# Double blocks of seven products in the first feed-forward, on rows scaled in place

## The chip, the core and the metric

The kernel runs on one core of a Trainium2 chip. Five engines work side by side, each through its own instructions in order: TensorE (PE, matmuls), VectorE (DVE), ScalarE (ACT), GpSimd (POOL) and SyncE (SP), which issues the DMA transfers. They wait for each other by semaphores. The metric is the device time of one execution in microseconds; before the change it is 1522.33 us, the median of 3 runs (1522.22 to 1524.28).

## What is computed

A decoder trunk of two layers on 256 rows of 1024 numbers, all in float32:

```
for i in range(2):
    x = x + 0.5 * swiglu(rmsnorm(x, norm_ffn1[i]), w_ffn1_up[i], w_ffn1_down[i])
    h = rmsnorm(x, norm_mix[i])
    x = x + token_mixers(h, ...)                      # three branches, gates, w_out
    x = x + 0.5 * swiglu(rmsnorm(x, norm_ffn2[i]), w_ffn2_up[i], w_ffn2_down[i])
    gate = sigmoid(rmsnorm(x, norm_ple[i]) @ w_ple_gate[i])
    x = x + gate * (p[i] @ w_ple_proj[i])
return rmsnorm(x, norm_final)

def rmsnorm(x, g): return x * rsqrt(mean(x * x) + 1e-6) * g
def swiglu(x, w_up, w_down):                          # w_up 1024 x 5632, w_down 2816 x 1024
    g, u = split(x @ w_up, 2)
    return (silu(g) * u) @ w_down
```

The change concerns the first line of layer 0.

## The kernel before

Every product is made of three matmuls of a faster type (L227 to L229): each operand is split into a part h, rounded to that type, and the rest l, and h·h, l·h and h·l are added in PSUM. A weight unit is 128 x 1024 numbers (512 KB): SyncE loads it into one of four buffers raw, ScalarE casts it to h (L221), VectorE subtracts (L222, l = raw - h). The h and l tiles come from pools of five, and of two more (ph, pl) while the wide pools are open. The rows of the input, transposed, are kept as xth and xtl, one pair for each half t of 128 rows.

A feed-forward runs over 11 blocks of 256 hidden numbers. A narrow block has 48 up matmuls (four units, two halves of rows), silu and product (hid: sg on ScalarE, hd on VectorE), the 24 down matmuls of the block before, and four transposes of hd (L468) whose result is split again (fh, fl). The last block transposes in two steps (L542). A wide, or double, block does two neighbouring blocks at once: a 2 x 2 product of matrices with seven products instead of eight, 84 up matmuls instead of 96. For this VectorE sums quarters of the weights (L385), ScalarE and VectorE split each sum (L377, L378), and four sums of the rows (sums_x) are split once in each feed-forward.

Three of the four feed-forwards have wide blocks at 2, 5 and 8. Their rows are normalised before they are split: xs is x times rstd (L300 on ScalarE, L301 on VectorE), eight transposes (L311) bring it into PSUM, VectorE multiplies by the gains into xr (L314), and ScalarE and VectorE split xr into xth and xtl. The first feed-forward of layer 0 gets x transposed from memory, multiplies by the gains alone, starts its matmuls before the rows' norm is known, and multiplies by rstd behind the product, in hid (L462, L463). Its eleven blocks are all narrow, and its wide pools are not open.

rstd comes from jk (L426: the squares' sum, ScalarE), ms (L431, VectorE) and a power on POOL (L432).

Between layer 0 and layer 1 stands the gate of the layer's embedding (ple): four products sq of 24 matmuls, one for each half of columns and rows; for each a sigmoid g on ScalarE (L596), a product with pp (L597) and the sum into x on VectorE (L598), and jk. Behind the third the first half of the rows is complete, and ms, rstd, xs and its transposes follow for the next feed-forward, whose first units are cast in the same stretch. In layer 1 the gate is the last step but the final norm.

The order on each engine is not written out by hand. A scheduler sets it from the order in which the program asks for work, from priorities and from the buffers that are free; the pools' rotation runs through the whole program.

Of the kernel before, what the change touches and what calls it, by code (L numbers as in the profile page):

```python
# [10 lines left out]
F32 = mybir.dt.float32  # L11
# [4 lines left out]
OP = mybir.AluOpType  # L16
# [6 lines left out]
FB = DFF // 256  # L23
# [41 lines left out]
SPLIT_AHEAD = 0  # L65
WIDE = (2, 5, 8)
LANES = {'a': 1, 'b': 1, 'c': 2}
# [16 lines left out]
def plan(name, i):  # L84
    if (name, i) == ("w_ffn1", 0):
        return [(False, b) for b in range(FB)]
    return [(b in WIDE, b) for b in range(FB) if b - 1 not in WIDE]

# [56 lines left out]
class Build:  # L145
# [183 lines left out]
    def mixer_open(self):  # L329
        self.scope = ExitStack()  # L330
        for n, bufs in (("ar1", 1), ("ar2", 1), ("pp_", 3), ("gt", 6)):
            setattr(self, n, self.scope.enter_context(self.tc.tile_pool(name=n, bufs=bufs, reuse_waits="tile")))

    def sums_x(self):
        nc = self.nc
# [101 lines left out]
    def ffn(self, name, gcol_next, mid=None, hook=None):  # L437
        nc = self.nc
        rstd = self.rstd
        scaled = (name, self.layer) != ("w_ffn1", 0)  # L440
        acc = {}
# [42 lines left out]

        for wide, b in plan(name, self.layer):
            if wide:
                hds = self.wide_up(name, b)
                downs()
                prev = []
                for j in range(2):  # L490
                    hh = self.fh.tile([128, 2, 256], F32R, name="fh")
                    ll = self.fl.tile([128, 2, 256], F32R, name="fl")
                    pt = self.pt.tile([128, 2, 256], F32, name="pt")
# [21 lines left out]
            for q, t in order:  # L515
# [4 lines left out]
                up(q, t)  # L520
            hds = [hid(pu, t) for t in range(2)]
            if b < FB - 1:
                if prev is not None:
# [4 lines left out]
                self.hl(hh, ll, pt)  # L528
                if scaled and b == 0:
                    self.sums_x()  # L530
            else:
# [614 lines left out]
    def constants(self):  # L1146
        nc, a = self.nc, self.a
# [21 lines left out]
        self.cols = cols = dict(zip(GAINS, (0, 16, 32, 48, 64, 80, 86)))  # L1169
        self.g_cq, self.g_ckv = cols["c_q_norm"], cols["c_kv_norm"]  # L1170
        self.mhalf = self.const.tile([128, 4], F32, name="mhalf")
        nc.vector.memset(self.mhalf, -0.5)
# [36 lines left out]
    def program(self, out):  # L1209
# [5 lines left out]
        cols = self.cols  # L1215
        self.norm_begin(cols["norm_ffn1"])

        def load_xt(t):
# [8 lines left out]
        def late(b):  # L1227
            if b == 2:
                self.load_consts()
                nc.gpsimd.dma_start(self.mask_b, a["const_i"])  # L1230
                self.load_gnorm()
                self.bounds()
# [14 lines left out]
        for i in range(DEPTH):  # L1247
            self.layer = i
            self.ffn("w_ffn1", cols["norm_mix"] + 8 * i, hook=self.late_loads if i == 0 else None)
            if i:  # L1250
                self.wide_close()
            self.mixer_open()
# [67 lines left out]
```

## Time and profile before

| | us |
|---|---|
| median of 3 runs | 1522.33 |
| profiled execution | 1522.07 |
| its span | 1519.8 |
| PE busy | 1490.3 (98%) |
| DVE busy | 1106.9 (73%) |
| ACT busy | 935.1 (62%) |
| POOL busy | 39.0 (3%) |
| DMA queue of SyncE | 263.00 MB, 51.5% of 16 engines' span |

A row of the timeline shows the start in us from the span's begin, the duration, engine, line, operation, output and inputs, shape, and how many such instructions follow each other; in brackets the idle time of the engine before it and what ended it. Matmuls overlap: a matmul of 128 x 512 shows a duration of 0.39 us, and the next one starts 0.23 us later. One row of a matmul in plain float32 stands for two records ("x2").

### The profile page before, as it was taken

To read this page: it belongs to the slowest core of one execution; us is meant where nothing else is said; L and a number is where in the kernel's file an instruction comes from. 1 tells how busy PE (TensorE), PEld (TensorE's weight loads), DVE (VectorE), ACT (ScalarE), POOL (GpSimd) and SP (SyncE) were. 2 spreads that over 40 slices of the span, in tenths; PEclk is the share of its full clock that TensorE was granted. 3 is DMA by queue.
4 is the path that set the end of the run, shared out by engine and by line. 5 is a ranking of instruction groups with operands and counts; after the bars stand their busy time and mean duration, and the time that the engine had idled before them with its cause. 6 is when DMAs were issued, how large, how long until landed. Compare 5 with 4: busy or idle time off the path is not lost.

```text
span 1519.8 us, 21607 instructions
## 1 busy us (share of the span) xinstructions
PE 1490.3 (98%) x8176; PEld 1242.5 (82%) x8176; DVE 1106.9 (73%) x1657; ACT 935.1 (62%) x1373; POOL 39.0 (3%) x48
## 2 busy tenths in 40 slices
PE   8999999999999999999989999999999999999997
PEld 6888888888888878888868888888888888788886
DVE  6555577677866679997679996776777666899965
ACT  6444486578655466756756665865885644666655
POOL 0000010000000000000000000100000000000000
PEclk9999999999999999999989999999999999999999
DMA  8665545454537652458534435553445285544462
GB/s 292 194 195 190 179 142 189 121 170 121 177 113 259 211 189 104 184 216 286 166 110 172 181 146 187 160 182 117 150 149 166 97 301 178 172 162 183 166 216 70
DMA packets 76472, 264.53 MB, mean 174 GB/s; under 512 B 8608, under 2 KB 9536, under 8 KB 76368
## 3 DMA queue, kind: packets, MB, share of 16 engines
q1 hardware_dynamic: 76144, 263.00, 51.5%
q8 instruction: 64, 1.05, 0.3%
q0 software_dynamic: 80, 0.11, 0.1%
q14 instruction: 40, 0.33, 0.1%
q10 hardware_dynamic: 144, 0.05, 0.0%
HBM read 262.08 MB, written 1.05 MB: 173 GB/s over the span
## 4 chain that ended last, share of the span: by engine, by line
PE 86%; ACT 7%; DVE 3%; DMA 2%; issue 2%; POOL 1%; SPq 0%; POOLq 0%; ACTq 0%; DVEq 0%
PE pu L227 19%; PE pu L229 19%; PE pu L228 19%; PE acc L229 5%; PE acc L227 5%; PE acc L228 5%; ACT h L221 2%; DMA raw<-in_weights_dram 2%; DVE l L222 1%; PE sq L229 1%; PE sq L227 1%; PE sq L228 1%; PE pt L468 1%; ACT P L696 1%; PE pt L254 1%
## 5 line engine op out<-in xcount | busy, mean ns | idle before, releaser
L222 DVE TENSOR_TENSOR l<-raw,h 128x1024 fp32r<-128x1024 f32 (+3 forms) x440 | 513.8, 1179 | 232.6 <-ACT h L221 226.4
L221 ACT CAST h<-raw 128x1024 fp32r<-128x1024 f32 (+4 forms) x439 | 439.3, 1011 | 237.0 <-PE pu L229 128.1
L227 PE MATMUL pu<-h,xth 128*128 128x512 f32 (+3 forms) x1160 | 450.2, 389 | 7.8 <-ACT xth L234 4.6
L228 PE MATMUL pu<-l,xth 128*128 128x512 f32 (+3 forms) x1160 | 442.0, 381 | 2.2 <-DVE l L222 2.2
L229 PE MATMUL pu<-h,xtl 128*128 128x512 f32 (+3 forms) x1160 | 439.8, 380 | 0.0
L227 PEld LDWEIGHTS pu<-h,xth 128*128 128x128 f32 x1160 | 218.9, 189 | 46.7 <-ACT xth L234 5.7
L228 PEld LDWEIGHTS pu<-l,xth 128*128 128x128 f32 x1160 | 219.0, 189 | 38.7 <-DVE l L222 5.1
L229 PEld LDWEIGHTS pu<-h,xtl 128*128 128x128 f32 x1160 | 218.5, 188 | 38.1 <-DVE xtl L235 1.4
L377 ACT CAST h<-wide 128x1024 fp32r<-128x1024 f32 x126 | 129.2, 1053 | 56.3 <-DVE wide L385 32.3
L378 DVE TENSOR_TENSOR l<-wide,h 128x1024 fp32r<-128x1024 f32 x126 | 148.0, 1219 | 1.3 <-ACT h L377 0.6
L229 PE MATMUL acc<-h,fl 128*128 128x512 f32 x352 | 137.8, 391 | 0.0
L228 PE MATMUL acc<-l,fh 128*128 128x512 f32 x352 | 137.2, 390 | 0.0
L227 PE MATMUL acc<-h,fh 128*128 128x512 f32 x352 | 136.7, 393 | 0.0
L385 DVE TENSOR_TENSOR wide<-wide 128x1024 f32<-128x1024 f32 x72 | 85.2, 1219 | 0.2
L229 PEld LDWEIGHTS acc<-h,fl 128*128 128x128 f32 x352 | 66.1, 188 | 13.7
L228 PEld LDWEIGHTS acc<-l,fh 128*128 128x128 f32 x352 | 66.2, 188 | 13.4
L227 PEld LDWEIGHTS acc<-h,fh 128*128 128x128 f32 x352 | 66.2, 188 | 13.2
L229 PE MATMUL pu<-h,sl 128*128 128x512 f32 x144 | 56.1, 390 | 0.0
L228 PE MATMUL pu<-l,sh 128*128 128x512 f32 x144 | 56.1, 390 | 0.0
L227 PE MATMUL pu<-h,sh 128*128 128x512 f32 x144 | 56.1, 389 | 0.0
L228 PE MATMUL pu<-l,fh 128*128 128x512 f32 x128 | 50.9, 397 | 0.0
L227 PE MATMUL pu<-h,fh 128*128 128x512 f32 x128 | 50.4, 394 | 0.0
(273 smaller groups left out, 1838.1 us busy)
## 6 DMA issues: line engine op xcount, KB each, us to landing
raw<-in_weights_dram SPq DMA_DIRECT2D x374, 512.0 KB, 4.4
wide<-in_weights_dram SPq DMA_DIRECT2D x72, 512.0 KB, 6.4
raw<-in_weights_dram SPq DMA_DIRECT2D x48, 384.0 KB, 3.4
raw<-in_weights_dram SPq DMA_DIRECT2D x8, 320.0 KB, 3.6
raw<-in_weights_dram SPq DMA_DIRECT2D x8, 256.0 KB, 2.7
xin<-in_xt_dram SPq DMA_DIRECT2D x4, 256.0 KB, 8.1
x<-in_x_dram SPq DMA_DIRECT2D x2, 512.0 KB, 9.9
out_dram<-o SPq DMA_DIRECT2D x4, 256.0 KB, 2.2
```

Source lines behind the costliest of these rows:

```text
L221: (copy or nc.scalar.copy)(h[:, :m], raw[:, :m])
L222: nc.vector.tensor_tensor(l[:, :m], raw[:, :m], h[:, :m].bitcast(F32), op=OP.subtract)
L227: mm(out, ah, bh, start=start, stop=False, skip_group_check=skip)
L228: mm(out, ah, bl, start=False, stop=False, skip_group_check=skip)
L229: mm(out, al, bh, start=False, stop=stop, skip_group_check=skip)
L254: nc.tensor.transpose(pt[:, k, :], src[:, half * 512 + k * 128:half * 512 + (k + 1) * 128], self.ident)
L377: nc.scalar.copy(h, src)
L378: nc.vector.tensor_tensor(l, src, h.bitcast(F32), op=OP.subtract)
L385: nc.vector.tensor_tensor(d[j][:, :, dh], d[j][:, :, dh], r[j][:, :, rh], op=OP.add)
L468: nc.tensor.transpose(pt[:, f, t * 128:(t + 1) * 128], hd[:, f * 128:(f + 1) * 128], self.ident)
L696: nc.scalar.activation(P[n, o], P[n, o], AF.Exp, bias=q[:, 3:4], scale=A_SCALE, accum_out=q[:, 4 + n:5 + n])
```

## The change

The first feed-forward of layer 0 gets wide blocks at 5 and 8. For them the rows must be normalised, which they are not at its start. Behind block 2 a new function scale_x adds xth and xtl to the raw rows again, builds rstd on a diagonal (dg = ident x rstd), spreads it over all partitions by a product with a matrix of ones, and multiplies the rows by it; sums_x follows. Behind the hid of block 4 split_x writes the split of the scaled rows over xth and xtl in place. Blocks above 4 use the form of hid without rstd. The wide pools open at the start of the program, with two more h and l tiles, and close after the first feed-forward in both layers; the weights of blocks 5, 6, 8 and 9 are packed for wide blocks; the loads of the remaining constants are asked for at block 3 instead of block 2.

```
-WIDE = (2, 5, 8)
+WIDE, WIDE_FIRST = (2, 5, 8), (5, 8)
+SCALE_AT = 4
...
 def plan(name, i):
-    if (name, i) == ("w_ffn1", 0):
-        return [(False, b) for b in range(FB)]
-    return [(b in WIDE, b) for b in range(FB) if b - 1 not in WIDE]
+    wide = WIDE_FIRST if (name, i) == ("w_ffn1", 0) else WIDE
+    return [(b in wide, b) for b in range(FB) if b - 1 not in wide]
...
+    def scale_x(self):
+        nc = self.nc
+        self.rawx = [self.xr.tile([128, 8, 128], F32, name=f"xr{t}", tag=f"xr{t}") for t in range(2)]
+        pt = self.pt.tile([128, 2, 128], F32, name="pt")
+        for t in range(2):
+            raw = self.rawx[t]
+            nc.vector.tensor_tensor(raw, self.xth[t].bitcast(F32), self.xtl[t].bitcast(F32), op=OP.add)
+            dg = self.tm.tile([128, 128], F32, name="dg", tag="tm")
+            nc.vector.tensor_scalar(dg, self.ident, self.rstd[t], None, op0=OP.mult)
+            nc.tensor.matmul(pt[:, t, :], self.ones, dg, start=True, stop=True)
+            nc.vector.tensor_tensor(raw, raw, pt[:, t, :].unsqueeze(1).to_broadcast([128, 8, 128]), op=OP.mult)
+
+    def split_x(self):
+        for t in range(2):
+            for g in (slice(0, 4), slice(4, 8)):
+                self.hl(self.xth[t][:, g, :], self.xtl[t][:, g, :], self.rawx[t][:, g, :])
...
     def ffn(self, name, gcol_next, mid=None, hook=None):
-        scaled = (name, self.layer) != ("w_ffn1", 0)
+        opening = (name, self.layer) == ("w_ffn1", 0)
+        scaled = not opening
...
         for wide, b in plan(name, self.layer):
+            scaled = not opening or b > SCALE_AT
...
             hds = [hid(pu, t) for t in range(2)]
+            if opening and b == SCALE_AT:
+                self.split_x()
             if b < FB - 1:
...
                 if scaled and b == 0:
                     self.sums_x()
+                if opening and b == SCALE_AT - 2:
+                    self.scale_x()
+                    self.sums_x()
...
+        self.ones = self.const.tile([128, 128], F32, name="ones")
+        nc.gpsimd.memset(self.ones, 1.0)
...
         self.norm_begin(cols["norm_ffn1"])
+        self.wide_open()
...
         def late(b):
-            if b == 2:
+            if b == 3:
...
             self.ffn("w_ffn1", cols["norm_mix"] + 8 * i, hook=self.late_loads if i == 0 else None)
-            if i:
-                self.wide_close()
+            self.wide_close()
             self.mixer_open()
```

The change also moves instructions far behind the first feed-forward. In the following pieces the lines of the changed kernel are others than before: L394, L395, L402 for L377, L378, L385; L443, L448 for L426, L431; L480 for L462; L620 to L622 for L596 to L598.

First ScalarE at blocks 4 and 5 of the first feed-forward; fh is the split of a narrow block's hidden numbers, wide a pair of raw units of a double block. Before:

```order
L221 CAST h<-raw 128x1024 x3
L462 ACTIVATE sg<-pu,rstd 128x256 x2
L221 CAST h<-raw 128x1024 x3
L234 CAST fh<-pt 128x512
L221 CAST h<-raw 128x1024 x3
```

Now, with xth and xtl rewritten from xr (xr0 and xr1 are the scaled rows of the two halves):

```order
L394 CAST h_884<-wide_869 128x1024
L234 CAST fh_633<-pt_727 128x512
L394 CAST h_894<-wide_872 128x1024
L234 CAST xth0_110<-xr0_552 128x512
L234 CAST xth1_111<-xr1_553 128x512
L394 CAST h_908<-wide_869 128x1024
L394 CAST h_918<-wide_872 128x1024
L234 CAST xth0_110<-xr0_552 128x512
L480 ACTIVATE sg_810<-pu_734,rstd_116 128x256
L234 CAST xth1_111<-xr1_553 128x512
L480 ACTIVATE sg_814<-pu_735,rstd_117 128x256
```

The four casts of split_x stand among the casts of wide 5 and the two sg of block 4.

Second ScalarE in the gate of layer 0's embedding; g is the sigmoid of a quarter, raw_7097 the first unit of layer 1's first feed-forward. Before:

```order
L237 ACTIVATE xth1_6662<-pt_6842,gains_99 128x128 x2
L221 CAST h_7099<-raw_7097 128x1024
L596 ACT_TABLE_LOAD
L596 ACTIVATE g_6919<-sq_6894,rstd_6667 128x512
L221 CAST h_6964<-raw_6962 128x1024
L221 CAST h_6970<-raw_6968 128x1024
L426 ACTIVATE jk_6923,ss_6866<-x_91 128x512
L221 CAST h_6976<-raw_6974 128x1024
L596 ACTIVATE g_6950<-sq_6925,rstd_6668 128x512
L221 CAST h_7105<-raw_7103 128x1024
```

Now, where that unit is raw_7196:

```order
L237 ACTIVATE xth1_6761<-pt_6941,gains_99 128x128
L620 ACT_TABLE_LOAD
L620 ACTIVATE g_7018<-sq_6993,rstd_6766 128x512
L221 CAST h_7063<-raw_7061 128x1024
L221 CAST h_7069<-raw_7067 128x1024
L443 ACTIVATE jk_7022,ss_6965<-x_91 128x512
L221 CAST h_7075<-raw_7073 128x1024
L620 ACTIVATE g_7049<-sq_7024,rstd_6767 128x512
L221 CAST h_7198<-raw_7196 128x1024
L443 ACTIVATE jk_7053,ss_6966<-x_91 128x512
```

The cast of the next feed-forward's first unit has moved from in front of the table load to behind the second g.

Third VectorE a little later in the same gate, from the third quarter's g to xs. Before:

```order
L597 TENSOR_TENSOR g_7005<-g_7005,pp_6780 128x512
L222 TENSOR_TENSOR l_7112<-raw_7109,h_7111 128x1024
L598 TENSOR_TENSOR x_91<-x_91,g_7005 128x512
L222 TENSOR_TENSOR l_7232<-raw_7229,h_7231 128x1024
L222 TENSOR_TENSOR l_7238<-raw_7235,h_7237 128x1024
L431 SCALAR_TENSOR_TENSOR ms_7011<-ss_6866 128x1
L222 TENSOR_TENSOR l_7244<-raw_7241,h_7243 128x1024
L301 TENSOR_SCALAR xs_7037<-x_91,rstd_6868 128x512
```

Now:

```order
L621 TENSOR_TENSOR g_7104<-g_7104,pp_6879 128x512
L622 TENSOR_TENSOR x_91<-x_91,g_7104 128x512
L222 TENSOR_TENSOR l_7205<-raw_7202,h_7204 128x1024
L448 SCALAR_TENSOR_TENSOR ms_7110<-ss_6965 128x1
L301 TENSOR_SCALAR xs_7136<-x_91,rstd_6967 128x512
L222 TENSOR_TENSOR l_7217<-raw_7214,h_7216 128x1024
```

Three differences of next units have moved from between g and xs to other places, one of them to directly behind xs.

## Rows read from the trace of the kernel before

**Rows 1.** The page: busy time of TensorE, and the chain by engine.
```profile
PE 1490.3 (98%) x8176; PEld 1242.5 (82%) x8176; DVE 1106.9 (73%) x1657; ACT 935.1 (62%) x1373; POOL 39.0 (3%) x48
...
PE 86%; ACT 7%; DVE 3%; DMA 2%; issue 2%; POOL 1%; SPq 0%; POOLq 0%; ACTq 0%; DVEq 0%
```

**Rows 2.** Timeline of TensorE: start, duration, operation, in two feed-forwards.
```profile
84.78 0.39 PE L227 MATMUL acc<-h,fh 128*128 128x512 f32 x1
...
90.23 0.60 PE L468 MATMUL pt<-ident,hd 128*128 128x128 f32 x4
...
185.61 0.38 PE L542 MATMUL pt<-ident,hd 128*128 128x128 f32 x2
...
629.67 0.60 PE L468 MATMUL pt<-ident,hd 128*128 128x128 f32 x4
...
719.45 0.38 PE L542 MATMUL pt<-ident,hd 128*128 128x128 f32 x2
```

**Rows 3.** Stretches: length, busy PE, PEld, DVE, ACT, POOL; clock, DMA, GB/s.
```profile
90.20:185.60 95.40, 95.40 (x433) 78.97 (x432) 49.67 (x52) 43.33 (x52) 0.00 (x0) 1.00 0.56 178
629.60:719.40 89.80, 89.80 (x409) 74.56 (x408) 77.79 (x78) 57.55 (x69) 0.00 (x0) 1.00 0.61 218
```

**Rows 4.** Groups by form: operation, count | busy us, mean ns | idle before.
```profile
L378 DVE TENSOR_TENSOR l<-wide,h 128x1024 fp32r<-128x1024 f32 x126 | 148.0, 1219 | 1.3 <-ACT h L377 0.6 <-DMA wide<-in_weights_dram 0.4
...
L235 DVE TENSOR_TENSOR xtl<-xr,xth 128x512 fp32r<-128x512 f32 x12 | 7.8, 686 | 0.2
L314 DVE TENSOR_TENSOR xr<-pt,gains 128x512 f32<-128x512 f32 x12 | 7.8, 684 | 6.2 <-PE pt L311 6.2
...
L234 ACT CAST xth<-xr 128x512 fp32r<-128x512 f32 x12 | 7.0, 616 | 2.5 <-DVE xr L314 2.5
```

**Rows 5.** Timeline of VectorE in the first microseconds.
```profile
11.91 1.23 DVE L222 TENSOR_TENSOR l<-raw,h 128x1024 fp32r<-128x1024 f32 x1 [1.99 <-ACT h L221]
```

**Rows 6.** Timeline of TensorE: plain float32 matmuls of branch C.
```profile
429.99 0.39 PE L1041 MATMUL psc<-knT,cbig 128*128 128x128 f32 x2
430.21 0.39 PE L1042 MATMUL psc<-kpeT,qpeT 128*128 128x128 f32 x2
```

**Rows 7.** Timeline of TensorE from layer 0's gate to layer 1.
```profile
759.81 0.39 PE L229 MATMUL sq<-h,xtl 128*128 128x512 f32 x1
765.67 1.97 PE L311 MATMUL pt<-ident,xs 128*128 128x128 f32 x8 [5.47 <-ACT xs L300]
768.21 0.79 PE L227 MATMUL pu<-h,xth 128*128 128x512 f32 x1 [0.58 <-ACT xth L234]
...
776.19 1.03 PE L311 MATMUL pt<-ident,xs 128*128 128x128 f32 x8
778.66 0.50 PE L227 MATMUL pu<-h,xth 128*128 128x512 f32 x1 [1.44 <-ACT xth L234]
```

**Rows 8.** A stretch behind that gap, columns as in rows 3.
```profile
768.30:777.00 8.70, 8.70 (x32) 6.65 (x32) 3.04 (x7) 2.64 (x5) 0.55 (x1) 0.73 0.09 38
```

**Rows 9.** Timeline of ScalarE in layer 0's gate.
```profile
744.93 1.05 ACT L221 CAST h<-raw 128x1024 fp32r<-128x1024 f32 x1 [1.83 <-DMA raw<-in_weights_dram]
...
756.26 1.05 ACT L221 CAST h<-raw 128x1024 fp32r<-128x1024 f32 x1 [0.33 <-DMA raw<-in_weights_dram]
757.22 0.68 ACT L596 ACTIVATE g<-sq,rstd 128x512 f32<-128x512 f32 x1
```

**Rows 10.** Timeline of VectorE and POOL, the norm behind that gate.
```profile
763.10 0.15 DVE L431 SCALAR_TENSOR_TENSOR ms<-ss 128x1 f32<-128x1 f32 x1
...
763.33 1.53 POOL L432 TENSOR_TENSOR rstd<-ms,mhalf 128x1 f32<-128x1 f32 x1 [28.33 <-DVE ms L431]
771.00 0.55 POOL L432 TENSOR_TENSOR rstd<-ms,mhalf 128x1 f32<-128x1 f32 x1 [6.14 <-DVE ms L431]
```

**Rows 11.** Timeline of ScalarE and TensorE before layer 0's second feed-forward.
```profile
544.37 1.05 ACT L221 CAST h<-raw 128x1024 fp32r<-128x1024 f32 x1 [3.16 <-DMA raw<-in_weights_dram]
...
548.19 1.09 PE L311 MATMUL pt<-ident,xs 128*128 128x128 f32 x8 [0.75 <-ACT xs L300]
```

## What I predict

> **What bounds the kernel now.** I read the page's busy shares first, then the chain of waits. TensorE is busy 98% of the 1519.8 us span and carries 86% of the chain [rows 1]; the span is bound by the number and spacing of matmuls, and what VectorE or ScalarE does counts only where a matmul waits for it. The profiled execution took 1522.07 us, 2.27 us more than its span and 0.26 us under the median of 1522.33; I sum against 1522.07.
>
> Next the timeline of TensorE, for the marks that every feed-forward leaves: the transposes of a narrow block (L468) and those of the last block (L542). From block 4's transposes to the first L542 the first feed-forward, all narrow, takes 185.61 - 90.23 = 95.38 us. The same stretch of layer 0's second feed-forward, with double blocks at 5 and 8, takes 719.45 - 629.67 = 89.78 us [rows 2]. TensorE is busy all the time in that second stretch, although VectorE is at 77.79 of 89.8 us [rows 3].
>
> Last the gaps of TensorE. One stands out: 5.47 us at 765.67, between the products of layer 0's gate (ple) and the first feed-forward of layer 1, ended by xs (L300) on ScalarE; behind it 24 matmuls need 776.19 - 768.21 = 7.98 us [rows 7], where 24 down matmuls of the first feed-forward need 90.23 - 84.78 = 5.45 [rows 2]. The granted clock there is 0.73 of full speed [rows 8]: a mean of TensorE's two levels, 1.2 GHz first, after it stood still, and 2.4 GHz again later.
>
> **The change, part by part.**
>
> *Two double blocks.* Each replaces 96 up matmuls by 84; what is saved is TensorE's time alone, and rows 2 give it whole, with the transposes of both forms: 95.38 - 89.78 = 5.60 us. It holds if wide 5 and 8 wait for nothing here either. New beside them stands split_x: four casts 128x512 on ScalarE (0.62 us each) and four subtractions on VectorE (0.69 each) between the last up product of block 4 and wide 5's first product, among the wide block's own L395 (1.22 us, L378 before) [rows 4] and L402, as large. In the changed order the four casts stand between wide casts and the two sg of block 4, the subtractions between the wide differences. Product a11 needs all of row-half 0 split. TensorE has 24 down matmuls of block 3 and block 4's transposes in front of it, 5.45 + 0.60 = 6 us [rows 2]. Walking ScalarE's and VectorE's new order with these durations I find the last operand some 3 us before a11, and those of the next products about 1 us before each. I cost split_x at nothing; if the cover fails, it is late by at most its own 4 x 0.69 = 2.8 us.
>
> *scale_x and sums_x behind block 2.* VectorE gets two sums 128x1024, two dg, two products 128x1024 from PSUM (twice L314's 0.68) and eight differences 128x512, ScalarE four casts: near 2 x 1.22 + 2 x 1.4 + 8 x 0.69 = 11 us on an engine that in this stretch works 49.67 of 95.40 us [rows 3, 4]. The first sum moves right to the start, into an idle time of 1.99 us at 11.91 [rows 5]; it fits, since it may begin when the last xtl is written (about 9.6) and takes 1.22. That costs nothing. TensorE gets two plain fp32 matmuls 128x128, and such a one shows as two records, and the next begins 0.22 us behind it (429.99, 430.21) [rows 6]: 0.45 us together, on the path. Both write one pt tile, so the second waits until VectorE has multiplied row-half 0; from the order I count 0 to 0.5 us of wait, and take 0.2. Bounds for the whole edit: 0.45 and, if both products of 1.4 us are waited for, 3.2.
>
> *wide_open at the start.* Two more pairs of h and l buffers serve the first feed-forward and eight loads of 512 KB find free buffers. TensorE waits for no buffer there between 40 and 185 us, so I cost it at nothing; the start has small gaps and could give or lose 0.3.
>
> *The order behind it.* The rotation of buffers shifts, and with it the order of casts up to the end. I compared each engine's order before and after; the one place where a difference meets a gap is 744 to 779. Before, ScalarE has a cast of a next unit in front of g#1, waiting 1.83 us for its transfer (744.93); g#3, the third of the gate's four quarters, comes at 757.22 [rows 9]; VectorE has two differences in front of ms (763.10), and one right behind it, beside which POOL's rstd takes 1.53 us instead of 0.55 [rows 10]; only then xs. After, the cast stands behind g#2, one difference stands in front of ms, and xs directly behind ms. Walking the new order with the durations of these rows: the first quarter's products end at 743.9, the table load follows at once, g#1 stands at 745.2 (2.1 earlier); the transfers that wait for VectorE's next differences come earlier with it, and g#3 stands at 755.0. Its two VectorE operations end at 757.4, jk on ScalarE 0.8 later, ms at 758.5, rstd 0.55, xs 759.3, and the transposes start at 760.1 instead of 765.67, 0.5 us behind the last product in front of them. The first up product follows 2.5 us later, as 768.21 follows 765.67 now: 762.6. One more difference stands in front of xtl: 0.85. 24 matmuls, 5.45: 768.9. The second xs is ready 0.7 later, and the matmul behind its transposes comes after another 2.5, as 778.66 after 776.19: 772.1 instead of 778.66, so 6.6 us earlier. With no long gap I let the clock stay full, as it is behind the 0.75 us at 548.19 [rows 7, 9 to 11]. Bounds: 0, if the gap is set by the transfers, and 5.47 + 0.58 + 1.44 for the gaps and 7.98 - 5.45 = 2.53 for the slow clock, 10.0 in all, if nothing waits there any more [rows 2, 7]. I take the 6.6 of the walk.
>
> **The sum.** 1522.07 - 5.60 + 0.45 + 0.2 - 6.6 = 1510.5 us: **1510.5**. More than half of the gain comes from a place that the change doesn't mention.
>
> **Rivals.**
>
> *B, the boundary stays as it is.* What ends the wait of 1.83 us at 744.93 is a transfer; if transfers come as late in the new order, g#3 hangs on its unit again (0.33 us at 756.26 was such a wait) [rows 9] and the gap stays. For it: loads are issued only when a difference frees a buffer. Against it: the units in front were on time, and the moved cast no longer stands on the chain. 1522.07 - 5.60 + 0.65 = 1517.1.
>
> *C, the gap goes but not the slow clock.* TensorE would still stand still four times and more between the last gate product and 772.1, by the walk 0.5, 1.2, 0.85 and 0.7 us besides the second transposes' 1.5. The rows show 1.44 at 778.66 and 0.75 at 548.19 [rows 7, 11], with matmuls at full spacing behind them, never so many in a row. If the clock falls, 24 matmuls cost 7.98 instead of 5.45 again: 1510.5 + 2.5 = 1513.0. The Trainium skill speaks for this rival: "TensorE: Matmul & The Clock Gate", section "A second HAM failure mode: psum-queue depth-cycling", has short idles between groups of matmuls sending the clock to and fro. By that rule the time would be 1513.0, by the rows 1510.5; no run shown so far has such a string of gaps.
>
> *D, slower: the stall comes back elsewhere.* At 544.37 a cast waits 3.16 us for its transfer, between the two jk that end in xs of layer 0's second feed-forward; TensorE waits only 0.75 for that xs [rows 11]. In the new order a cast of a unit stands ahead of both jk, and another between them and xs. If both wait for their transfers, 3.16 us and the time of one more 512 KB at 218 GB/s [rows 3], 2.4, xs comes 5.6 us later, and behind a gap like that of 765.67 the clock falls too: 5.6, 0.9 for eight transposes (1.97 instead of 1.03) [rows 7] and 2.5 for the matmuls, 9.0. The kernel is slower by this only if the boundary at 765.67 isn't mended either: 1517.1 + 9.0 = 1526.1. It decides once xs there is over 5 us late. Against it: the cast that moves up belongs to a load that was issued earlier.
>
> *E, the double blocks don't give what they say.* split_x on two in-order engines, VectorE already busy 77.79 of 89.8 us in such a stretch [rows 3], delays products s1 to s4 of wide 5 by about 1.2 us each, 5 us in all, and the boundary stays: 1522. Against it: the margin of 1 us, and 45 us of VectorE idle in the stretch before.
>
> **Chances.** My forecast 0.50 (1508 to 1512.3), C 0.16, B 0.21, E 0.06, D 0.07. What a measurement tells from no change is 0.2%, 3 us: faster than 1519.3 in the first three cases, 0.87; same 0.06; slower 0.07. The range goes from 1507.5 (nearly all of the 10.0 at the boundary) to 1518.5 (B with 1.4 us of waits at split_x or the dg products); it leaves out D, E and the tails, some 0.18.
>
> **What would show it.** Block 4's transposes to L542 in the first feed-forward at 89.8 to 90.5 us, with TensorE busy all the time; two short pairs of matmuls (L343) in block 3 with under 0.5 us of wait; the transposes of xs behind layer 0's gate products within 1 us of the last product, and the clock full behind them. Wrong would be: a wait for L395, L235 or L394 at wide 5 of over 1 us; a gap of over 3 us for xs at any boundary; or a stretch from L542 to the last gate products of layer 0 that is over 1 us longer than now.

## The result, and the profile after

| | before | after |
|---|---|---|
| median, us | 1522.82 (4 runs, 1522.22 to 1524.28) | 1514.34 (4 runs, 1511.45 to 1514.99) |
| ratio, 95% interval | | 0.9942 [0.9930, 0.9954] |
| profiled execution, us | 1522.07 | 1514.13 |
| its span, us | 1519.8 | 1512.3 |

The change makes the kernel 8.5 us faster by the medians; the ratio says 8.8 (7.0 to 10.7). The forecast was 1510.5; the time lies 3.8 us above it and inside the range.

The page of the changed kernel, against [rows 1]: TensorE keeps its 86% of the chain and has 20 matmul records and 6.1 us of work less (24 matmuls fewer, and four records for the two products with dg).

```profile
PE 1484.2 (98%) x8156; PEld 1236.6 (82%) x8156; DVE 1151.8 (76%) x1705; ACT 954.4 (63%) x1397; POOL 38.2 (3%) x49
...
PE 86%; ACT 7%; DVE 3%; issue 2%; DMA 2%; POOL 0%; SPq 0%; POOLq 0%; ACTq 0%; DVEq 0%
```

The timeline of TensorE in the changed kernel, with the marks that answer to [rows 2] (L486 was L468, L566 was L542; start, duration, operation):

```profile
56.26 0.60 PE L486 MATMUL pt<-ident,hd 128*128 128x128 f32 x4
56.69 0.39 PE L343 MATMUL pt<-dg,ones 128*128 128x128 f32 x2
...
59.27 0.49 PE L343 MATMUL pt<-dg,ones 128*128 128x128 f32 x2
...
73.69 0.60 PE L486 MATMUL pt<-ident,hd 128*128 128x128 f32 x4
...
90.50 0.60 PE L486 MATMUL pt<-ident,hd 128*128 128x128 f32 x4
...
180.28 0.38 PE L566 MATMUL pt<-ident,hd 128*128 128x128 f32 x2
```

Block 4's transposes to the last block's: 180.28 - 90.50 = 89.78 us, to the hundredth the same stretch of layer 0's second feed-forward before [rows 2]. Between 56.26 and 73.69 stand the two products with dg (L343); block 2's transposes to block 4's take 90.50 - 56.26 = 34.24 instead of 33.61 us.

The stretch of the double blocks, with the columns of [rows 3]:

```profile
90.50:180.30 89.80, 89.80 (x410) 74.55 (x409) 76.03 (x77) 56.42 (x68) 0.00 (x0) 1.00 0.49 176
```

TensorE is busy all of it, at the full clock; so split_x is hidden.

The timeline of the changed kernel where layer 0's gate ends, which answers to [rows 7, 10] (VectorE's ms, POOL's rstd, then TensorE):

```profile
752.91 0.15 DVE L448 SCALAR_TENSOR_TENSOR ms<-ss 128x1 f32<-128x1 f32 x1
753.14 0.55 POOL L449 TENSOR_TENSOR rstd<-ms,mhalf 128x1 f32<-128x1 f32 x1 [23.07 <-DVE ms L448]
754.50 1.09 PE L311 MATMUL pt<-ident,xs 128*128 128x128 f32 x8 [1.12 <-ACT xs L300]
...
756.90 0.50 PE L227 MATMUL pu<-h,xth 128*128 128x512 f32 x1 [0.84 <-ACT xth L234]
...
758.33 0.50 PE L229 MATMUL pu<-h,xtl 128*128 128x512 f32 x1 [0.70 <-DVE xtl L235]
...
758.91 0.57 PE L228 MATMUL pu<-l,xth 128*128 128x512 f32 x1
...
759.71 0.63 PE L227 MATMUL pu<-h,xth 128*128 128x512 f32 x1
760.13 0.63 PE L228 MATMUL pu<-l,xth 128*128 128x512 f32 x1
...
762.27 0.45 PE L227 MATMUL pu<-h,xth 128*128 128x512 f32 x1
```

The gap of 5.47 us is 1.12, and rstd takes 0.55 instead of 1.53. But around 760 the matmuls stand 0.42 us apart instead of 0.23. The granted clock of that stretch is 0.69 of full speed, a mean of the two levels 1.2 and 2.4 GHz:

```profile
756.90:762.30 5.40, 4.70 (x13) 3.43 (x14) 5.40 (x8) 2.71 (x5) 0.00 (x0) 0.69 0.62 196
```

The eight steps from 758.91 to 762.27 take 3.36 us, at full spacing 8 x 0.227 = 1.82: this is rival C, and it costs 1.5 us. Behind 762.27 the spacing is full again.

The last place that differs much is one that the prediction doesn't name: layer 1, from its mixer's last products (sq) to its second feed-forward. Four sums add these products to x there (L1137, now L1161); behind the third, half of the rows is complete, and jk, ms, rstd, xs and its transposes follow. Between the sums VectorE has differences of weight units (L222). First the kernel before, its timeline of VectorE and TensorE:

```profile
1285.81 0.69 DVE L1137 TENSOR_TENSOR x<-x,sq 128x512 f32<-128x512 f32 x1 [0.52 <-PE sq L229]
1288.30 3.95 DVE L222 TENSOR_TENSOR l<-raw,h 128x1024 fp32r<-128x1024 f32 x3 [1.80 <-ACT h L221]
1292.16 0.68 DVE L1137 TENSOR_TENSOR x<-x,sq 128x512 f32<-128x512 f32 x1
1292.76 1.22 DVE L222 TENSOR_TENSOR l<-raw,h 128x1024 fp32r<-128x1024 f32 x1
1294.19 1.23 DVE L222 TENSOR_TENSOR l<-raw,h 128x1024 fp32r<-128x1024 f32 x1 [0.21 <-ACT h L221]
1296.69 0.69 DVE L1137 TENSOR_TENSOR x<-x,sq 128x512 f32<-128x512 f32 x1 [1.27 <-PE sq L229]
1298.16 0.16 DVE L431 SCALAR_TENSOR_TENSOR ms<-ss 128x1 f32<-128x1 f32 x1 [0.79 <-ACT jk L426]
...
1299.81 1.09 PE L311 MATMUL pt<-ident,xs 128*128 128x128 f32 x8
```

TensorE doesn't wait there. Now the changed kernel, with the last of ScalarE's casts and jk:

```profile
1275.17 0.69 DVE L1161 TENSOR_TENSOR x<-x,sq 128x512 f32<-128x512 f32 x1 [0.54 <-PE sq L229]
1277.55 1.22 DVE L222 TENSOR_TENSOR l<-raw,h 128x1024 fp32r<-128x1024 f32 x1 [1.69 <-ACT h L221]
1279.12 3.50 DVE L222 TENSOR_TENSOR l<-raw,h 128x1024 fp32r<-128x1024 f32 x3 [0.34 <-ACT h L221]
1282.53 0.68 DVE L1161 TENSOR_TENSOR x<-x,sq 128x512 f32<-128x512 f32 x1
1283.67 1.23 DVE L222 TENSOR_TENSOR l<-raw,h 128x1024 fp32r<-128x1024 f32 x1 [0.46 <-ACT h L221]
1286.44 1.05 ACT L221 CAST h<-raw 128x1024 fp32r<-128x1024 f32 x1 [2.18 <-DMA raw<-in_weights_dram]
1287.52 1.23 DVE L222 TENSOR_TENSOR l<-raw,h 128x1024 fp32r<-128x1024 f32 x1 [2.62 <-ACT h L221]
1288.66 0.68 DVE L1161 TENSOR_TENSOR x<-x,sq 128x512 f32<-128x512 f32 x1
1289.38 0.63 ACT L443 ACTIVATE jk<-x 128x512 f32<-128x512 f32 x1 [1.89 <-DVE x L1161]
1290.13 0.16 DVE L448 SCALAR_TENSOR_TENSOR ms<-ss 128x1 f32<-128x1 f32 x1 [0.79 <-ACT jk L443]
...
1291.74 1.09 PE L311 MATMUL pt<-ident,xs 128*128 128x128 f32 x8 [2.08 <-ACT xs L300]
```

Read it upward: TensorE waits 2.08 us for xs, which hangs on ms, ms on jk, and jk on the third of the four sums. That sum stands on VectorE behind a difference which waits 2.62 us for a cast, and the cast waits 2.18 us for its transfer. In VectorE's order before, three differences stand between the first sum and the second, two between the second and the third, none between that and ms: five. In the changed order they are four, two and none: the sixth belongs to a unit that hasn't landed when VectorE comes to it.

All stretches of the two profiled executions, from marks of TensorE's timeline, in us:

| stretch | before | after | difference | forecast |
|---|---|---|---|---|
| start to block 2's transposes | 56.62 | 56.26 | -0.36 | 0 |
| to block 4's | 33.61 | 34.24 | +0.63 | +0.65 |
| to L566 | 95.38 | 89.78 | -5.60 | -5.60 |
| to layer 0's second feed-forward | 374.59 | 373.53 | -1.06 | 0 |
| that feed-forward | 159.25 | 159.32 | +0.07 | 0 |
| gate, to layer 1's first block | 59.78 | 55.00 | -4.78 | -6.6 |
| layer 1's first feed-forward | 159.39 | 159.42 | +0.03 | 0 |
| to its second | 373.19 | 376.20 | +3.01 | 0 |
| that feed-forward | 159.32 | 159.31 | -0.01 | 0 |
| the rest, with what lies outside the span | 50.94 | 51.07 | +0.13 | 0 |
| sum | 1522.07 | 1514.13 | -7.94 | -11.55 |

("to its second" means the first transposes of its block 0.) The two terms of the change's own text came out to 0.02 us. What went another way is the order far behind it: 1.8 us less gained at the gate than forecast, 3 us lost at a boundary of layer 1, 1.1 gained at one of layer 0 (its gap of 0.75 us [rows 11] is gone). The start and that 1.1 were not in the sum; without them the profiled execution would lie 5 us above the forecast instead of 3.6.

### The profile page after: what moved, and what is told of

It is laid out like the page before. It is cut to its first block, busy times and chain, and to the rows that moved or that the text cites. A ratio compares the mean times of both kernels' runs of the same rounds, so it can differ in the third digit from the quotient of the medians.

```text
span 1512.3 us, 21640 instructions
## 1 busy us (share of the span) xinstructions
PE 1484.2 (98%) x8156; PEld 1236.6 (82%) x8156; DVE 1151.8 (76%) x1705; ACT 954.4 (63%) x1397; POOL 38.2 (3%) x49
## 3 DMA queue, kind: packets, MB, share of 16 engines
q8 instruction: 64, 1.05, 0.3%
HBM read 262.08 MB, written 1.05 MB: 174 GB/s over the span
## 4 chain that ended last, share of the span: by engine, by line
PE 86%; ACT 7%; DVE 3%; issue 2%; DMA 2%; POOL 0%; SPq 0%; POOLq 0%; ACTq 0%; DVEq 0%
PE pu L227 19%; PE pu L229 19%; PE pu L228 19%; PE acc L229 5%; PE acc L227 5%; PE acc L228 5%; ACT h L221 2%; DMA raw<-in_weights_dram 2%; DVE l L222 2%; PE sq L228 1%; PE sq L227 1%; PE sq L229 1%; PE pt L486 1%; ACT P L720 1%; PE pt L254 1%
## 5 line engine op out<-in xcount | busy, mean ns | idle before, releaser
L222 DVE TENSOR_TENSOR l<-raw,h 128x1024 fp32r<-128x1024 f32 (+3 forms) x424 | 494.7, 1178 | 184.7 <-ACT h L221 179.1
L221 ACT CAST h<-raw 128x1024 fp32r<-128x1024 f32 (+3 forms) x423 | 423.1, 1009 | 195.9 <-PE pu L229 99.2
L227 PE MATMUL pu<-h,xth 128*128 128x512 f32 (+3 forms) x1112 | 430.6, 388 | 8.0 <-ACT xth L234 5.0
L228 PE MATMUL pu<-l,xth 128*128 128x512 f32 (+3 forms) x1112 | 423.0, 380 | 2.3 <-DVE l L222 2.2
L229 PE MATMUL pu<-h,xtl 128*128 128x512 f32 (+3 forms) x1112 | 420.5, 379 | 1.1 <-DVE xtl L235 1.1
L394 ACT CAST h<-wide 128x1024 fp32r<-128x1024 f32 x154 | 157.7, 1052 | 70.7 <-DVE wide L402 35.7
L395 DVE TENSOR_TENSOR l<-wide,h 128x1024 fp32r<-128x1024 f32 x154 | 181.1, 1224 | 3.4 <-ACT h L394 2.4
L402 DVE TENSOR_TENSOR wide<-wide 128x1024 f32<-128x1024 f32 x88 | 104.2, 1221 | 0.3
L227 PE MATMUL pu<-h,sh 128*128 128x512 f32 x176 | 68.5, 389 | 0.0
L229 PE MATMUL pu<-h,sl 128*128 128x512 f32 x176 | 68.5, 389 | 0.0
```

The costliest lines, as they stand in the source:

```text
L221: (copy or nc.scalar.copy)(h[:, :m], raw[:, :m])
L222: nc.vector.tensor_tensor(l[:, :m], raw[:, :m], h[:, :m].bitcast(F32), op=OP.subtract)
L227: mm(out, ah, bh, start=start, stop=False, skip_group_check=skip)
L228: mm(out, ah, bl, start=False, stop=False, skip_group_check=skip)
L229: mm(out, al, bh, start=False, stop=stop, skip_group_check=skip)
L394: nc.scalar.copy(h, src)
```

## The experiments

The order behind the first feed-forward depends on the change in one way only: by how many steps the rotation of the seven h and l tiles is shifted (self.turn, which counts modulo 7). The two double blocks shift it by minus 2. Starting the count elsewhere gives the changed kernel the old order, or the old kernel the new one: in the traces VectorE's instructions from the mixer of layer 0 to the end then stand in the same sequence. So blocks and order can be separated. Gains are given by the ratios to before, with their intervals; a profile is one execution.

**Double blocks, old order.** The changed kernel, with

```
-        self.more, self.turn = False, 0
+        self.more, self.turn = False, 2
```

> The changed kernel with one number different: the rotation of the h and l tiles starts at 2 instead of 0, which gives back the order of before on every engine from the mixer of layer 0 to the end. Theory 1 (two parts that add: the double blocks, and the order that the shifted rotation makes): scaling costs 0.63 for its two matmuls and their wait, the start gives 0.4, two wide blocks give 5.6, and the boundary behind layer 0's gate keeps its gap of 5.5 us: 5.4 us under the kernel before, 1517.4. Theory 2 (the gain is the double blocks' own, the order behind them is worth nothing): as the changed kernel, 8.5 us under, 1514.3.

1516.73 us (6 runs, 1514.98 to 1520.43), ratio to before 0.9966 [0.9954, 0.9977]. Its gate keeps a gap of 4.48 us, and layer 1's boundary has none. So the blocks themselves give 5.2 us (3.5 to 7.0; 6.1 by the medians), beside a term of 5.60 - 0.65 = 4.95. The profiled execution, 1520.43, is the longest of the six: its start up to block 2 takes 3.4 us more than before, of which the section on the hardware has more.

**Old plan, new order.** The kernel before with turn = 5, no double block in the first feed-forward.

> The kernel before with one number different: the rotation of the h and l tiles starts at 5 instead of 0, which gives the order of the changed kernel from the mixer of layer 0 to the end; all blocks of the first feed-forward stay narrow. Theory 1: the gap behind layer 0's gate falls from 5.5 to about 1.1 us (4.8 less in all by the traces of before and after), layer 0's mixer gives 1.1, the boundary before layer 1's second feed-forward loses 2.8 by a gap of 2.1 for xs, the end loses 0.5: 2.6 us under the kernel before, 1520.2. Theory 2: within 0.5 us of before, 1522.8.

1519.60 us (11 runs, 1516.39 to 1521.54), ratio 0.9977 [0.9969, 0.9986]: 3.5 us from the order alone (2.1 to 4.7; 3.2 by the medians). The gate takes 53.13 us, 6.65 less than before, which is the walk of the prediction with the clock full; the mixer of layer 0 gives 1.24; the boundary of layer 1 loses 4.45. It gets a gap of 3.09 us, and behind that even the eight transposes take 1.97 us instead of 1.09 (granted clock 0.86 from 1295 to 1307); the timeline of TensorE:

```profile
1295.47 1.97 PE L311 MATMUL pt<-ident,xs 128*128 128x128 f32 x8 [3.09 <-ACT xs L300]
```

-6.65 - 1.24 + 4.45 = -3.4, and 3.5 was measured. With the 5.2 of the blocks the two halves make 8.7, and the change 8.8.

**Scaling alone.** The changed kernel with

```
-WIDE, WIDE_FIRST = (2, 5, 8), (5, 8)
+WIDE, WIDE_FIRST = (2, 5, 8), ()
```

which scales and splits the rows but has only narrow blocks.

> The changed kernel with no wide block in the first feed-forward: rows are scaled, summed and split in place, then used by narrow blocks; its order behind is that of before. Theory 1: scaling costs only TensorE's time for two short matmuls, 0.63 us, the start gives 0.4: +0.2 us, 1523.0, the same. Rival: the scaling is paid for by waits, up to 3.2 us, 1526.

1521.54 us (11 runs, 1520.74 to 1524.74), ratio 1.0001 [0.9992, 1.0009]. Block 2 to block 4 takes 91.21 - 57.00 = 34.21 us, the narrow stretch 95.38 as before: scale_x costs 0.6 us and split_x nothing.

**Splitting twice.** A second split_x right behind the first.

```
+                self.split_x()
```

> The changed kernel with split_x done twice (four more casts of 0.62 us and four more differences of 0.69). Theory 1 (the split is hidden, with 3 us to spare before a11 and about 1 us at the sums' products): the stretch from block 4's transposes to L566 grows from 89.78 by 0 to 1.8 us. Rival (the split stands on the edge): it grows by 2.8 us, and by more if the clock falls.

1514.45 us (5 runs, 1513.24 to 1516.11), ratio 0.9948 [0.9936, 0.9961]. The stretch from block 4 takes 89.90 us, against 89.78 and 89.87 in the two profiles of the changed kernel. Four more casts and four more differences cost 0.1 us at most: the cover that the prediction names holds for twice the work.

**One double block.** WIDE_FIRST = (5,) with turn = 1, which restores the old order.

> The changed kernel with a wide block at 5 only, and the rotation started at 1, which gives the order of before behind the first feed-forward. Theory 1: half of the double blocks' gain, 2.8, less 0.2 for the scaling: 2.6 us under before, 1520.2. Rival: the first double block pays for the split in place (it waits for its rows), and gives under 1 us, 1522.

1522.05 us (11 runs, 1520.95 to 1524.22), ratio 0.9997 [0.9988, 1.0005]; the time was missed by 1.9 us. Its timeline of TensorE:

```profile
58.52 0.60 PE L486 MATMUL pt<-ident,hd 128*128 128x128 f32 x4
...
92.74 0.60 PE L486 MATMUL pt<-ident,hd 128*128 128x128 f32 x4
...
185.37 0.38 PE L566 MATMUL pt<-ident,hd 128*128 128x128 f32 x2
```

185.37 - 92.74 = 92.63, 2.75 less than narrow: half of the gain, as expected. The time is the rival's, 1522, but its reason, a double block that waits for its rows, is not what this stretch shows. What is missing in the profile lies ahead of block 2, which ends 1.9 us later than before; the section on the hardware has that start. That it explains all 11 runs can't be seen from one profile.

**A third order.** The changed kernel with turn = 1, in whose order layer 1's boundary has three differences between the first two sums again.

> The changed kernel with the rotation of the h and l tiles started at 1: on VectorE layer 0's gate keeps the changed kernel's order, and layer 1's boundary before its second feed-forward gets back the order of before, with three differences instead of four between the first sum into x and the next. Theory 1 (what the change lost against my sum is mainly that boundary): the stretch from layer 1's L566 to the first L486 of its second feed-forward goes from 376.2 to about 373.5 us, the gate's stretch stays at 53 to 55: 2.7 us under the changed kernel, 1511.6. Rival (late transfers set that gap, whatever stands in front of xs): a gap of 2 us or more stays, 1514.3.

1515.92 us (5 runs, 1513.38 to 1516.26), ratio 0.9953 [0.9940, 0.9967]: a miss. Layer 1's gap falls to 1.21 us, but layer 0's second feed-forward gets one (timeline of ScalarE, VectorE and TensorE):

```profile
541.86 1.05 ACT L221 CAST h<-raw 128x1024 fp32r<-128x1024 f32 x1 [4.13 <-DMA raw<-in_weights_dram]
542.94 1.23 DVE L222 TENSOR_TENSOR l<-raw,h 128x1024 fp32r<-128x1024 f32 x1 [2.55 <-ACT h L221]
545.68 1.97 PE L311 MATMUL pt<-ident,xs 128*128 128x128 f32 x8 [2.83 <-ACT xs L300]
```

It is the same chain: in this order four, one and one differences stand up to ms, six again; the sixth waits for a cast, and the cast 4.13 us for its transfer. The stall had moved with the order, to rival D's place: 2.83 us of gap, and 1.97 us for the transposes instead of 1.09.

**A fourth order.** turn = 4, an order with five differences up to ms at both boundaries.

> The changed kernel with the rotation of the h and l tiles started at 4: VectorE never has four differences between the first and second sum into x, at neither of the boundaries before a second feed-forward, and layer 0's gate keeps the changed kernel's order. Theory 1 (four differences there hold up xs, by 2 to 3 us, in the layer where the rotation puts them: layer 1 in the changed kernel, layer 0 in the third order): gaps for xs of under 1.3 us at all three boundaries, from L566 to the first L486 about 373.5 us in layer 0, 53 to 55 over the gate, 373.9 in layer 1: 2.5 us under the changed kernel, 1512.0. Rival (one of the boundaries always pays): a gap of 2 us or more at one, 1514.5.

1511.35 us (5 runs, 1509.27 to 1513.64), ratio 0.9925 [0.9913, 0.9938], expected 1512.0. Its transposes of xs, on TensorE's timeline:

```profile
545.03 1.09 PE L311 MATMUL pt<-ident,xs 128*128 128x128 f32 x8
...
756.94 1.09 PE L311 MATMUL pt<-ident,xs 128*128 128x128 f32 x8 [0.51 <-ACT xs L300]
...
1291.29 1.09 PE L311 MATMUL pt<-ident,xs 128*128 128x128 f32 x8 [1.30 <-ACT xs L300]
```

No gap above 1.3 us at any of the three. Against before the gate gives 6.98 us, layer 0's mixer 1.21, and layer 1's boundary costs 1.63 instead of 3.01; with the change's own terms that makes 11.5 us, the sum that the prediction wanted, now measured as 11.4. This leaves out the start: the profiled execution, the longest of the five, is only 8.4 us under the one before, as its start takes 2.9 us more. The expectation came from counting VectorE's differences between the first two sums alone, three or four; four go with six up to ms in every profile here. Over all 14 profiles, the eight boundaries before a second feed-forward with six differences have gaps of 1.97 to 3.09 us, and the twenty with five have at most 1.30. The interval overlaps the changed kernel's, so the times alone don't make the 3 us between the two certain; the gaps do show where they are from.

**A later sum.** In the profile of the changed blocks in the old order VectorE's first sum of scale_x stands in front of a difference that TensorE waits for (its rows are in the section on the hardware). To bring the sum behind rstd, in the third order (turn = 1):

```
+            zero = self.small.tile([128, 1], F32, name="zero", tag="zero")
+            nc.vector.tensor_scalar(zero, self.rstd[t], 0.0, None, op0=OP.mult)
-            nc.vector.tensor_tensor(raw, self.xth[t].bitcast(F32), self.xtl[t].bitcast(F32), op=OP.add)
+            nc.vector.scalar_tensor_tensor(raw, self.xth[t].bitcast(F32), zero, self.xtl[t].bitcast(F32), op0=OP.add, op1=OP.add)
```

> As the run before it, and the sum xth + xtl of scale_x waits for rstd (it adds rstd x 0 as well), so that it stands behind the last weight differences of block 0 instead of in front of the second one. Theory: where the rows' transfer lands late, the early sum delays the difference that TensorE waits for by up to 1.2 us, and the clock may fall behind it; without it the start up to block 0's transposes takes 22.4 us in every profile: 0.5 us under the run before on the median, 1511.1. Rival: the sum was hidden by the idle 1.99 us, no difference (within 0.3 us), or 1 us more since the second sum now stands in front of hd of block 0.

1527.43 us (5 runs, 1526.42 to 1529.84), ratio 1.0035 [1.0022, 1.0047]: slower by 11.5 us than the same order without it, a plain miss. The start takes 2.3 us more in its profile, and the gap before layer 0's second feed-forward 0.2; the rest is no wait: the matmuls themselves stand further apart, a narrow block takes 16.98 us instead of 16.80 and each of the three later feed-forwards some 2.5 us more, at the full clock. The new tile has a place of its own, four copies of 32 bytes, and every buffer behind it lies 128 bytes further (the compiled program's addresses: fh from 132992 to 133120). Three runs follow that up.

The same idea without a new place, in the fourth order (turn = 4), the zero taken from block 1's fl and kept in the tile of ms; the sum itself is changed as above:

```
+            zero = self.small.tile([128, 1], F32, name="zero", tag="ms")
+            nc.vector.tensor_scalar(zero, late[:, 0, 0:1].bitcast(F32), 0.0, None, op0=OP.mult)
```

> The fourth order, and the sum xth + xtl of scale_x waits for block 1's hidden numbers (it adds 0 times one of them), so that it leaves the first 40 us; its small tile takes a place of the tag ms, so that no buffer moves. Theory: matmuls at the usual spacing (16.8 us from L486 to L486 in narrow blocks, not the 17.0 of the first late sum, which had moved every later buffer by 128 bytes); the start up to block 0's L486 shorter in the mean, as the early sum no longer stands in front of a difference that TensorE waits for: 0.5 us under the fourth order, 1511.5. Rivals: spacing 1% longer again (then the late sum itself does it, 1525); or no gain at the start.

1510.46 us (5 runs, 1509.39 to 1512.81), ratio 0.9922 [0.9909, 0.9936]. A narrow block takes 16.79 us again; against the fourth order alone (0.9925) no gain can be told. It is the fastest version here by its median.

The changed kernel with nothing but an unused tile:

```
+        self.pad = self.small.tile([128, 1], F32, name="pad", tag="pad")
```

> The changed kernel with one unused tile of 128 x 1 numbers in the pool small: the same instructions in the same order, every buffer behind that pool 128 bytes further on. Theory (the 1% of the first late sum came from the moved buffers): matmuls at 0.2295 us instead of 0.2268, 13 us over the changed kernel, 1527. Rival (it came from something else in that program): as the changed kernel, 1514.5.

1526.66 us (8 runs, 1524.45 to 1528.22), ratio 1.0026 [1.0015, 1.0036], 12 us over the changed kernel. And the same tile with 128 x 32 numbers, which takes four times the place, so that the buffers move by 512 bytes:

> The changed kernel with an unused tile of 128 bytes for each of its four copies, so that every buffer behind it stands 512 bytes further instead of the 128 bytes of the run before; instructions and their order are the changed kernel's. Theory P (what counts is where the buffers that the matmuls read stand within a step of 512 bytes: 128 bytes change that, 512 bytes restore it; the kernel before has these buffers 512 bytes lower and shows the full spacing): a narrow block takes 16.80 us again, the time is that of the changed kernel, 1514.5 us (1511.5 to 1516.5). Rival Q (any shift to higher addresses, or the unused tile itself, costs the 1%): a narrow block takes 17.0 us, 1527 us.

1514.07 us (5 runs, 1512.76 to 1515.12), ratio 0.9940 [0.9927, 0.9954]: the changed kernel's time to 0.3 us. TensorE's transposes of blocks 1 and 2, moved by 128 bytes:

```profile
42.81 0.60 PE L486 MATMUL pt<-ident,hd 128*128 128x128 f32 x4
...
59.83 0.60 PE L486 MATMUL pt<-ident,hd 128*128 128x128 f32 x4
```

and moved by 512:

```profile
42.45 0.60 PE L486 MATMUL pt<-ident,hd 128*128 128x128 f32 x4
...
59.24 0.60 PE L486 MATMUL pt<-ident,hd 128*128 128x128 f32 x4
```

17.02 against 16.79 us for the same instructions. Rival Q falls: a larger shift by the same kind of tile costs nothing. Theory P fits, except that its step of 512 bytes is not shown; two shifts can't tell it from a step of 256. The miss of e6 came from the placement, not from the late sum.

**The changed kernel again**, for a second profile of it.

> The changed kernel once more, to see what differs between its runs. Theory: two places where TensorE stands still for a short time, the first 15 us and the boundary behind layer 0's gate, are followed in some runs by matmuls at 1.2 GHz and in others not, worth 1.5 to 4 us each; median 1514.3, runs between 1511 and 1516, and the runs with the lower mean clock are the longer ones. Rival: the runs differ by the transfers alone: no relation to the clock.

1514.58 us (5 runs, 1513.51 to 1515.68), ratio 0.9949 [0.9937, 0.9962]. The gate takes 53.29 us with the clock full (gaps of 0.91, 0.84 and 0.69), layer 1's boundary has a gap of 2.64, and the start is 2.6 us later than in the first profile. So the slow clock at the gate is no property of the kernel, and the stall of layer 1 is one. The longer runs do have the lower clock here, 0.996 in the two of 1515.7 us and 0.997 to 0.998 in the other three; whether the clock or a late transfer comes first these means don't say.

## Why the prediction was right, and where not

*Two double blocks, -5.60.* Right: 89.78 us in the trace, half of it with one block, and a time 5.2 us shorter (3.5 to 7.0) with the order held.

*dg and its wait, 0.45 + 0.2.* Right: 0.63 in the trace, 0.60 where the scaling stands alone. Ten up matmuls, 10 x 0.227 = 2.3 us, stand between the two pairs, which begin 2.6 us apart (56.69 and 59.27), so there is next to no wait in it.

*split_x at nothing.* Right, with room for twice as much. Rival E falls with it: no product of wide 5 waits.

*wide_open and the start at nothing, give or take 0.3.* Not settled: block 2's transposes come 0.36 us earlier in the first profile and 1.9 later in the second, 58.54; the section on the hardware has more.

*The boundary behind the gate, -6.6.* The walk was right: 6.65 with the old plan in the new order, 6.5 in the second profile of the changed kernel. Its steps were right too: it puts the first transposes 760.1 - 719.45 = 40.65 us behind L542, and the old plan in the new order has them at 758.85 - 717.94 = 40.91. The gap of 5.47 us is down to between 0.5 and 1.4 in every profile of a new order. The first profile shows 4.78, mostly because rival C took 1.5 us. The prediction priced C at 2.5 for 24 slow matmuls; eight were slow. By "TensorE: Matmul & The Clock Gate" of the Trainium skill, section "A second HAM failure mode: psum-queue depth-cycling", frequent short idles between groups of matmuls send the clock to and fro. The first profile agrees (1.12, 0.84 and 0.70 us, then 0.69 of full speed), the others don't: the run with buffers moved by 128 bytes has 1.37, 0.84 and 0.70 there, in its window

```profile
766.00:772.90 6.90, 6.05 (x24) 4.35 (x24) 6.17 (x9) 3.43 (x7) 0.55 (x1) 1.00 0.67 218
```

and stays full. What decides between them is open. So the sign that the prediction named, transposes within 1 us of the last product and a full clock behind them, came in the second profile (0.91 us, 1.00) and not in the first.

*Rival B* falls: no profile of a new order keeps the gap, and the three of the old order that have the scaling keep it (4.48, 3.98 and 5.28 us). *Rival D* had the right mechanism and the wrong place. The prediction looked at the boundary before layer 0's second feed-forward, counted the casts there, and never walked the same boundary of layer 1, where the kernel before has no gap and the sum has nothing. "The one place where a difference meets a gap" was the failing step: a new order must be walked where it may open a gap, not only where one stands. For the profiled execution the account closes: 1514.13 - 1510.5 = 3.6, of which 3.0 are that place, 1.8 the gate, -1.1 and -0.4 the mixer of layer 0 and the start, 0.2 the rest. The stall is that of the changed order: the old plan in that order has it (3.09), the blocks in the old order do not.

## What to carry to other kernels

A local change in a scheduled program can shift every later rotation of its buffers; hold the rotation and vary it alone to price both, and walk every boundary of the new order, those without a gap first. Count the loads whose work stands on an in-order engine ahead of what TensorE waits for: a sixth difference, whose unit had not landed, cost a gap of 2 to 3 us here, and up to 4.5 us in all where the clock fell behind it. And when a small edit makes everything 1% slower with no new wait, look at the addresses of the buffers before looking at the edit.

## What the hardware showed unexpectedly

*Placement.* 128 bytes of shift cost 12 us, 512 cost nothing, and the kernel before has the same buffers 512 bytes lower at the full spacing. Casts (1.05 us) and differences (1.23) keep their durations; only matmuls step further apart, some by 0.23 to 0.24 us instead of 0.227. The compiled programs' addresses, laid beside the timelines, show which: xth, xtl and five of the seven h and l tiles lie in front of the pool and don't move. From 40 to 180 us matmuls that read only these keep a median step of 0.227 us, if none beside them reads another; those that read a moved buffer (fh and fl, the sums of the rows, the other two h and l tiles) go from 0.227 to 0.231. So it is the reading of a moved buffer that costs. In the slow version these buffers begin at multiples of 512 bytes, in the others 384 bytes past one; whether that is the reason wasn't tried.

*The start.* The first transposes of block 0 begin between 22.3 and 26.3 us in the profiles. In the late ones (24.9 us and more) ScalarE waits over 3 us for the rows' transfer (xin), and the clock is low behind it (0.50 to 0.73 of full speed from 14 to 20 us); where the sum L340 is early, it stands in front of the first differences on VectorE. The timeline of the changed blocks in the old order:

```profile
9.90 1.28 ACT L237 ACTIVATE xth<-xin,gains 128x128 fp32r<-128x128 f32 x4 [3.53 <-DMA xin<-in_xt_dram]
11.59 1.22 DVE L340 TENSOR_TENSOR xr<-xth,xtl 128x1024 f32<-128x1024 f32 x1
12.74 2.35 DVE L222 TENSOR_TENSOR l<-raw,h 128x1024 fp32r<-128x1024 f32 x2
14.01 0.80 PE L228 MATMUL pu<-l,xth 128*128 128x512 f32 x1 [1.34 <-DVE l L222]
```

and its window:

```profile
14.00:20.00 6.00, 5.99 (x14) 4.74 (x15) 5.96 (x18) 5.46 (x17) 0.16 (x1) 0.50 1.03 407
```

0.50 of full speed is 1.2 GHz. In the first profile of the changed kernel the sum begins earlier, and TensorE waits less:

```profile
9.30 1.22 DVE L340 TENSOR_TENSOR xr<-xth,xtl 128x1024 f32<-128x1024 f32 x1
...
12.85 0.50 PE L228 MATMUL pu<-l,xth 128*128 128x512 f32 x1 [0.76 <-DVE l L222]
```

The sum isn't the cause: with it moved away, in the fourth order, the wait falls from 1.25 to 0.62 us, and block 0's transposes still begin at 25.73. Without the scaling they begin at 22.97 and 22.72 (two profiles); with it at 22.3 to 24.1 in three and 24.9 to 26.4 in nine. So the change may make a late start more likely, which two profiles don't settle; the term "start 0" would then be too small by some 2 to 3 us in the executions that have it. Not all do: in seven of the nine late profiles the profiled execution is the longest of its kernel's runs, and in none of the three early ones. That fits runs of one kernel that differ by 2 to 6 us in part by their start, and profiles that often show the longest; the runs without a profile don't show their start. What delays xin is open; the loads that the early opening of the wide pools allows were not tried by themselves.
